# Halving the product of queries and gates in a linear-attention layer

## The chip, the core and the metric

One core of a Trainium2 chip runs the kernel. Its engines are TensorE (PE in the profile; PEld is its weight load), VectorE (DVE), ScalarE (ACT), GpSimd (POOL) and SyncE (SP), which issues the transfers. The metric is the device time of one execution in microseconds (us).

## What is computed

One step of a two-layer decoder trunk over 1024 prompt tokens and 32 sample tokens (8 sequences of 4). Layer 0 is a gated recurrent block, layer 1 an HGRN2 layer: linear attention with a gate for each of the 128 key channels of each of its 8 heads. Cut to what matters here:

```python
def _hgrn2_chunked(q, k, v, log_g, S0):        # for each head
    cum = jnp.cumsum(gc, axis=2)                                     # log gates summed over a chunk's tokens
    inter = jnp.einsum('bhtk,bhkv->bhtv', qc * jnp.exp(cum), S)      # queries decayed from the chunk's start
    attn = jnp.einsum('bhtk,bhsk,bhtsk->bhts', qc, kc, decay)        # decay = exp(cum_t - cum_s), t >= s
    intra = jnp.einsum('bhts,bhsv->bhtv', attn, vc)
    S_new = jnp.exp(last)[..., None] * S + jnp.einsum('bhsk,bhsv->bhkv', kc * jnp.exp(last - cum), vc)

def _hgrn_layer(x, g_norm, w_in, lb, o_gain, w_out, S0):
    q, f, iv, gate = jnp.split(u, 4, axis=-1)                        # u = rmsnorm(x) @ w_in
    q = jax.nn.silu(q)
    log_g = jnp.logaddexp(jnp.log(lbh), jnp.log1p(-lbh) + jax.nn.log_sigmoid(f))
    k = -jnp.expm1(log_g)
```

## The kernel before

Activations lie with channels on the 128 partitions and the 1056 tokens (`TOK`; `HT` is 528, `QT` 264) along the free axis. Matrix products are made of three matmuls each (`mm3`, lines 243 to 245), from a high and a low part of both operands, which ACT and POOL split off (`whi` by a cast, `wlo` by the subtraction on line 323).

**Layer 1, head by head.** For head `h` the input projection gives the queries (row A), the gate (`Gs`, in the buffer named ST), the keys 1 - gate (row B), the values and the output gate. The decayed attention is built by levels of 1, 2, 4 up to 64 tokens. The queries stand in two rows: `arow(h, 0)` as they are, and `arow(h, 1)` multiplied by each token's own gate. `own_gate(h)` makes that second row (the buffer named R) from the first and from Gs in one DVE instruction over all 1056 tokens, line 1064. Then each level multiplies half of a row by the gates up to there (`scale`, lines 1034 and 1043; ACT copies the other half, line 1037), and PE makes the small 32-token blocks of the level from the rows (`diag`, line 1052).

PE's small blocks come in four bursts for each head, `burst1` to `burst4`, between the projection's large products. `burst1(h)` holds `levels01(h)`: 32 products of 32 tokens of row B by both rows A of the same tokens, so it is the first reader of what `own_gate` writes. `burst3(h)` holds `levels816(h)`, whose second part (line 1106) reads rows that `scale` made.

**Heads 0 and 1** are projected in three chunks of 352 tokens (`CH`). Head 0's queries and gates are made as the last work of layer 0 (`first1`, lines 714 to 720), the others by `item` (ACT's tanh on line 1007, POOL's gate and key rows on lines 1010 and 1012, DVE's silu on line 1016). While they run, DVE and POOL also build the sums of activations (`build`, the adds on line 1368) that the later heads' projection uses. **Heads 2 to 7** are projected by `seven`, seven products instead of eight over quarters of 264 tokens: sums of products are collected on DVE in buffers named k (`plus`, line 1501) and finished by `settle`, on ACT (tanh, line 1509; gates, line 1510; tanh of the queries, line 1515) and DVE (line 1516). Large products go to 3 PSUM banks in turn, the small ones to 5.

**What sets the order.** Nothing is issued in the order of the code. Class `Flow` records each operation with its engine, an estimated duration and the keys that it reads and writes; `plan` lays them out engine by engine, by a due time that `back` works out from the plan before, and the best plan of nine is emitted. Here PE's large and small products are one chain whose order is fixed. The others stand where their due times put them, so a change of one operation's cost or keys can move others. Which instruction waits for which is then settled by the regions of the buffers that each reads and writes.

Of the kernel before, what the change touches and what calls it, by code (L numbers as in the profile page):

```python
# [19 lines left out]
ALU = mybir.AluOpType  # L20
# [20 lines left out]
TOK = SEQ + NB * NS  # L41
# [7 lines left out]
HT, QT = TOK // 2, TOK // 4  # L49
# [162 lines left out]
def tile_trunk(ctx: ExitStack, tc: tile.TileContext, xT, prm, hc, w0, wg, wo0, w1, wo1, s_in,  # L212
               yT, h_out, c_out, sp_out, ss_out):
    nc = tc.nc
    V, S, G, T, Q = nc.vector, nc.scalar, nc.gpsimd, nc.tensor, nc.sync
# [80 lines left out]
    with ExitStack() as l0:  # L296
# [18 lines left out]
        def dve(n, emit, r, w, prio=5, both=False):  # L315
            fl.add("DVE", 0.13 + 0.0011 * n, emit, r, w, prio, both=both)
# [610 lines left out]
    with ExitStack() as l1:  # L927
# [27 lines left out]
        Bs, Gs, B2, VT, Gc = a_rows[0], ST, rows[2], rows[0], rows[4]  # L955
# [13 lines left out]
        def arow(h, i):  # L969
            return (R[:, 1], eight("A1")) if i else (R[:, 0 if h % 2 else 2], eight("A", h % 2))  # L970
# [4 lines left out]
        GK = [("G", x) for x in range(4)]  # L975
# [85 lines left out]
        def own_gate(h):  # L1061
            decay[h] = Gs, *GK
            (a, k0), (a1, k1) = arow(h, 0), arow(h, 1)
            dve(TOK, lambda: V.tensor_tensor(a1, a, Gs, op=ALU.mult), (*k0, *GK), k1, 1, True)

        def levels01(h, s, sk):
            av = R[:, 0:2] if h % 2 else R[:, 1:3]
# [450 lines left out]

        dma(si.rearrange("p b v -> p (b v)"), s_in[0], (), two("si"), 4, 512)
        own_gate(0)  # L1520
        spots = [(R[:, 3, i * QT:i * QT + QT], ("tmp", 2 + i)) for i in range(4)]
        small_ = [(tmp[:, i], ("tmp", i)) for i in range(2)]
# [3 lines left out]
        for h in range(HC):  # L1526
            order = [item(h, i) for i in ((0, 1, 3, 2) if h else (3, 2))]
            seq_ = [(i, c) for i in range(len(order)) for c in range(NCH)]
            if h == HC - 1:
                seq_ = seq_[:-6] + [(len(order) - 2 + i, c) for c in (2, 1, 0) for i in (0, 1)]  # L1530
            ws2 = {} if h else ahead
            for n, (i, c) in enumerate(seq_):
                if i not in ws2:
                    ws2[i] = weights(order[i][0], 1024)
                order[i][1](c, *product(ws2[i], xcols(c)))
                if h and n == 5:
                    own_gate(h)
                for j, b in enumerate((burst1, burst2, burst3, burst4)):
                    if n == (SPOTS0, SPOTS)[h][j]:
                        b(h if j < 2 else h - 1)  # L1540
# [15 lines left out]
        for h in range(HC, H):  # L1556
            seven(h, 0, 1, FQ0 if h == HC else FQ, (lambda h=h: burst3(h - 1), lambda h=h: burst4(h - 1)))
            own_gate(h)
            seven(h, 3, 2, GV, (lambda h=h: burst1(h), lambda h=h: burst2(h)))
# [7 lines left out]
        for k in range(H):  # L1567
            if k < 4:
                olds = [("x", 1, k, x) for x in range(2)] + [("T", 1, i, k, x) for i in range(2) for x in range(2)]
            else:  # L1570
                n, i = ((2, 0), (3, 0), (4, 0), (4, 1))[k - 4]
# [241 lines left out]
```

## Time and profile before

| | |
|---|---|
| time, median of 3 runs (lowest, highest) | 1061.53 us (1061.51, 1062.03) |
| profiled execution: its own time, its span | 1061.78 us, 1060.0 us |
| PE busy, share of the span | 1050.5 us, 99% |
| DVE busy | 843.0 us, 80% |
| ACT busy, POOL busy | 588.7 us, 542.4 us |
| mean granted clock of TensorE | 0.996 |
| `own_gate` (line 1064) | 8 instructions, 12.2 us in total |

The span runs from the first to the last instruction; 1.78 us of the execution's own time lie around it. Layer 1 begins at about 500 us of the span, heads 2 to 7 are projected from about 593 to 957 us, and the output projection's end follows. PE matmuls overlap, so a row shows a matmul for longer than the distance to the next one.

### The profile page before, as it was taken

The page shows a single profiled execution, that of the slowest core. Times are in us where ns is not written, and L with a number is a line of the kernel's source. Part 1 is how long each engine was busy: PE and PEld are TensorE (multiplying, and loading weights), DVE is VectorE, ACT ScalarE, POOL GpSimd, SP SyncE. Part 2 cuts the span into 40 slices and gives each one's busy share as a digit, 9 for nine tenths or more (in the row PEclk, how much of TensorE's full clock was granted, in tenths as well). Part 3 has the DMA queues.
Part 4 walks back from the last instruction along what each step waited for, and adds up shares of the span by engine and source line. Part 5 has one row for each costly group of instructions (what it writes and reads, how often), then busy time and mean ns, then how long its engine had stood idle before and what let it go on. Part 6 is the DMA issues. An engine that isn't in the chain of part 4 may idle for free.

```text
span 1060.0 us, 25683 instructions
## 1 busy us (share of the span) xinstructions
PE 1050.5 (99%) x9966; PEld 1024.3 (97%) x9966; DVE 843.0 (80%) x1677; ACT 588.7 (56%) x1329; POOL 542.4 (51%) x604
## 2 busy tenths in 40 slices
PE   9999999999999999999999999999999999999997
PEld 9999999999999999999999999999999999999996
DVE  7999996888888689265799988978979797985435
ACT  6568656877765875243354474646464545652323
POOL 3425443444534366555667555555545565651544
PEclk9999999999999999999999999999999999999998
DMA  9211112123852595440211121212121222355204
GB/s 301 64 27 45 54 51 74 57 61 100 241 157 64 174 298 164 124 136 28 71 47 36 44 101 45 94 42 92 41 86 54 73 71 73 107 177 167 86 1 164
DMA packets 70121, 103.07 MB, mean 97 GB/s; under 512 B 9200, under 2 KB 51184, under 8 KB 70000
## 3 DMA queue, kind: packets, MB, share of 16 engines
q1 hardware_dynamic: 67696, 98.67, 30.0%
q10 hardware_dynamic: 2304, 2.77, 0.8%
q8 instruction: 78, 1.28, 0.5%
q14 instruction: 43, 0.35, 0.1%
HBM read 71.05 MB, written 25.49 MB: 91 GB/s over the span
## 4 chain that ended last, share of the span: by engine, by line
PE 89%; DVE 7%; POOL 1%; DMA 1%; issue 1%; ACT 0%; ACTq 0%; POOLq 0%; DVEq 0%
PE mm L243 24%; PE mm L244 24%; PE mm L245 24%; PE hg L567 1%; PE hg L1052 1%; PE hg L1161 1%; PE hg L1271 1%; DVE R L1368 1%; DMA wraw<-in_w_dram 1%; PE hg L1217 1%; PE hg L243 1%; PE hg L244 1%; PE hg L245 1%; PE hg L1273 1%; DVE tmp L1368 1%
## 5 line engine op out<-in xcount | busy, mean ns | idle before, releaser
L243 PE MATMUL mm<-xh,whi 128*128 128x352 f32 (+1 forms) x1143 | 358.6, 314 | 0.0
L245 PE MATMUL mm<-xh,wlo 128*128 128x352 f32 (+1 forms) x1143 | 353.1, 309 | 0.0
L244 PE MATMUL mm<-xl,whi 128*128 128x352 f32 (+1 forms) x1143 | 353.1, 309 | 0.0
L323 POOL TENSOR_TENSOR wlo<-wraw,whi 128x256 fp32r<-128x256 f32 (+3 forms) x184 | 202.7, 1118 | 178.5 <-ACT whi L378 80.7
L244 PEld LDWEIGHTS mm<-xl,whi 128*128 128x128 f32 x1143 | 215.0, 188 | 1.5
L243 PEld LDWEIGHTS mm<-xh,whi 128*128 128x128 f32 x1143 | 214.7, 188 | 1.5
L245 PEld LDWEIGHTS mm<-xh,wlo 128*128 128x128 f32 x1143 | 214.8, 188 | 0.0
L499 DVE SCALAR_TENSOR_TENSOR k<-xb,prm_sb,k 128x352 f32<-128x352 f32 (+2 forms) x144 | 89.7, 634 | 10.4 <-ACT k L496 5.7
L243 PE MATMUL mm<-t,whi 128*128 128x264 f32 (+1 forms) x306 | 89.3, 292 | 0.0
L244 PE MATMUL mm<-t,whi 128*128 128x264 f32 (+1 forms) x306 | 87.7, 287 | 0.0
L245 PE MATMUL mm<-t,wlo 128*128 128x264 f32 (+1 forms) x306 | 87.5, 286 | 0.0
L1501 DVE TENSOR_TENSOR k<-mm,k 128x264 f32<-128x264 f32 x144 | 60.3, 427 | 20.5 <-PE mm L245 17.4
L323 POOL TENSOR_TENSOR wlo<-R,whi 128x256 fp32r<-128x256 f32 x64 | 60.0, 958 | 24.6 <-ACT whi L1428 24.6
L582 POOL TENSOR_TENSOR k<-X 128x352 f32<-128x352 f32 x36 | 45.8, 1281 | 47.5 <-DVE R L583 38.6
L378 ACT CAST whi<-wraw 128x512 fp32r<-128x512 f32 (+2 forms) x83 | 46.2, 574 | 30.5 <-PE mm L244 19.4
L243 PEld LDWEIGHTS mm<-t,whi 128*128 128x128 f32 x306 | 57.6, 188 | 0.2
L245 PEld LDWEIGHTS mm<-t,wlo 128*128 128x128 f32 x306 | 57.7, 188 | 0.0
L244 PEld LDWEIGHTS mm<-t,whi 128*128 128x128 f32 x306 | 57.6, 188 | 0.0
L1428 ACT CAST whi<-wraw 128x512 fp32r<-128x512 f32 x52 | 32.0, 618 | 36.2 <-PE mm L245 16.7
L243 PE MATMUL mm<-yh,whi 128*128 128x352 f32 x153 | 49.9, 326 | 0.0
L245 PE MATMUL mm<-yh,wlo 128*128 128x352 f32 x153 | 49.4, 323 | 0.0
L244 PE MATMUL mm<-yl,whi 128*128 128x352 f32 x153 | 49.4, 323 | 0.0
(479 smaller groups left out, 2636.5 us busy)
## 6 DMA issues: line engine op xcount, KB each, us to landing
wraw<-in_w_dram SPq DMA_DIRECT2D x90, 256.0 KB, 2.9
wraw<-in_wo_dram SPq DMA_DIRECT2D x34, 192.0 KB, 2.5
si<-in_s_in_dram SPq DMA_DIRECT2D x8, 512.0 KB, 3.6
out_ss_out_dram<-si SPq DMA_DIRECT2D x8, 512.0 KB, 2.6
R<-in_w_dram SPq DMA_DIRECT2D x15, 256.0 KB, 2.6
sg<-x1b SPq DMA_DIRECT2D x21, 176.0 KB, 3.1
x<-sg SPq DMA_DIRECT2D x21, 176.0 KB, 1.8
R<-td SPq DMA_DIRECT2D x72, 44.0 KB, 1.9
```

Source lines behind the costliest of these rows:

```text
L243: T.matmul(out, wh, xh, start=first, stop=False)
L244: T.matmul(out, wh, xl, start=False, stop=False)
L245: T.matmul(out, wl, xh, start=False, stop=last)
L323: emit = lambda: e.tensor_tensor(b, x, a.bitcast(F32), op=ALU.subtract)
L378: act(m, lambda hi=hi, raw=raw, m=m: S.copy(hi[:, :m], raw[:, :m]), rk, (hk,), prio)
L499: dve(u, lambda src=src, dst=dst, sh=sh, k=k: V.scalar_tensor_tensor(dst, sh(src, k), pc("cw", 12 * k + m), dst, op0=ALU.mult, op1=ALU.add ...
L567: fl.add("PE", 0.62, lambda ps=ps, i=i, c=c: T.matmul(ps[:96, :CH], gs[:, i, :], ST[:96, chunk(c)], start=True, stop=True), (("gs",), *((" ...
L582: pool(CH, lambda x=x, a=a, b=b: G.tensor_tensor(x, a.bitcast(F32), b.bitcast(F32), op=ALU.add), (ak, bk), (xk,), 3)
L1052: T.matmul(ps[32 * j:32 * j + 32, n * w:n * w + w], B[:, o:o + 32], q(slice(o, o + 32)), start=True, stop=True, tile_position=(0, 32 * j))
L1368: dve(n, lambda: V.tensor_tensor(o, a, b, op=op), r, (w,), prio, True)
L1428: act(512, lambda: S.copy(hi, raw), (rk,), (hk,), 2)
L1501: dve(QT, lambda: V.tensor_tensor(o[0], z[0], u[0], op=ALU.add), (z[1], u[1]), (o[1],), 0)
```

## The change

`own_gate(h)` becomes two DVE instructions, one for tokens 0 to 527 and one for tokens 528 to 1055. Each is recorded with the keys of its own half: two of the four quarters of the gates, and the same quarters of both query rows. In heads 2 to 7 the quarters have writers of their own, so each half can be placed by itself. In head 1 every chunk of the projection is recorded as writing all quarters, and both halves are recorded behind the last of them. Head 0's rows were written in layer 0's recording, which layer 1's `Flow` does not know.

```diff
         def own_gate(h):
             decay[h] = Gs, *GK
             (a, k0), (a1, k1) = arow(h, 0), arow(h, 1)
-            dve(TOK, lambda: V.tensor_tensor(a1, a, Gs, op=ALU.mult), (*k0, *GK), k1, 1, True)
+            for i in range(2):
+                u = slice(i * HT, i * HT + HT)
+                half = lambda k: [*k[2 * i::4], *k[2 * i + 1::4]]
+                dve(HT, lambda u=u: V.tensor_tensor(a1[:, u], a[:, u], Gs[:, u], op=ALU.mult), (*half(k0), *GK[2 * i:2 * i + 2]), half(k1), 1, True)
```

The three added lines shift the lines below: the new instructions are on line 1067, and what was line 1501 is line 1504.

PE's order is the same in both programs. On DVE, where head 0's rows come in at the end of layer 0 (line 715 finishes the last chunk of its queries; ST is the gate, line 1043 begins the products of neighbouring gates), before and after the change:

```order
L715 SCALAR_TENSOR_TENSOR R<-R,mm 128x352
L1064 TENSOR_TENSOR R<-R,ST 128x1056
L961 MEMSET ssq 128x9
L1043 TENSOR_TENSOR sg<-ST 128x528
L1043 TENSOR_TENSOR sg<-sg 128x264
```

```order
L1067 TENSOR_TENSOR R<-R,ST 128x528
L715 SCALAR_TENSOR_TENSOR R<-R,mm 128x352
L1067 TENSOR_TENSOR R<-R,ST 128x528
L961 MEMSET ssq 128x9
L1043 TENSOR_TENSOR sg<-ST 128x528
```

The first half went ahead of the last chunk of the queries, and the second half stands where the whole stood.

On DVE in head 1 (line 1368, later 1371, is `build`'s adds, line 1016 the silu of a chunk of the output gate, read from PSUM, line 1056 keeps a level's blocks), before and after:

```order
L1368 TENSOR_TENSOR tmp<-tmp,xl 128x264
L1064 TENSOR_TENSOR R<-R,ST 128x1056
L1043 TENSOR_TENSOR sg<-ST 128x528
L1016 SCALAR_TENSOR_TENSOR sg<-k,mm 128x352
L1043 TENSOR_TENSOR sg<-sg 128x264
L1056 COPY_PREDICATED attnd<-mask_86,hg 128x256
```

```order
L1371 TENSOR_TENSOR tmp<-tmp,xl 128x264
L1067 TENSOR_TENSOR R<-R,ST 128x528 x2
L1016 SCALAR_TENSOR_TENSOR sg<-k,mm 128x352
L1043 TENSOR_TENSOR sg<-ST 128x528
L1043 TENSOR_TENSOR sg<-sg 128x264
L1056 COPY_PREDICATED attnd<-mask_86,hg 128x256
```

Both halves stand in the place of the whole, and the silu came ahead of the first product of gates.

On DVE in head 4, which stands for heads 3 to 6 (line 1501, later 1504, takes a large product out of PSUM into k; line 1516, later 1519, finishes the second half of the queries; line 1438, later 1441, combines weights), before and after:

```order
L1501 TENSOR_TENSOR k<-mm,k 128x264
L1516 SCALAR_TENSOR_TENSOR R<-R,k 128x264
L1120 COPY attn<-mm 64x4x64
L1438 TENSOR_TENSOR wraw<-wraw 128x512
L1516 SCALAR_TENSOR_TENSOR R<-R,k 128x264
L1064 TENSOR_TENSOR R<-R,ST 128x1056
L1501 TENSOR_TENSOR k<-mm,k 128x264
L1043 TENSOR_TENSOR sg<-ST 128x528
```

```order
L1504 TENSOR_TENSOR k<-mm,k 128x264
L1067 TENSOR_TENSOR R<-R,ST 128x528
L1519 SCALAR_TENSOR_TENSOR R<-R,k 128x264
L1123 COPY attn<-mm 64x4x64
L1519 SCALAR_TENSOR_TENSOR R<-R,k 128x264
L1067 TENSOR_TENSOR R<-R,ST 128x528
L1441 TENSOR_TENSOR wraw<-wraw 128x512
L1504 TENSOR_TENSOR k<-mm,k 128x264
L1043 TENSOR_TENSOR sg<-ST 128x528
```

The first half went ahead of the two pieces of the second half's queries, the second half stands right behind them, and the weights' combination moved behind it; the next product is taken out of PSUM behind the same work as before.

## The prediction

> **What bounds the kernel now.** I read the page first, then the busy time by stretches of layer 1, then the waits of PE and of its weight load, then the chain of work that ended last.
>
> ```profile
> PE 1050.5 (99%) x9966; PEld 1024.3 (97%) x9966; DVE 843.0 (80%) x1677; ACT 588.7 (56%) x1329; POOL 542.4 (51%) x604
> ```
>
> PE is busy for 99% of the span. The question is therefore not how much work DVE is spared, but where PE still waits for it. The stretches of layer 1 (heads 0 and 1, heads 2 to 7, the last bursts, the end), with columns length, PE, PEld, DVE, ACT, POOL:
>
> ```profile
> 500.00:590.00 90.00, 88.97 (x1095) 86.57 (x1094) 78.31 (x150) 37.56 (x89) 60.42 (x58) 1.00 0.15 46
> 590.00:957.00 367.00, 367.00 (x5167) 354.16 (x5166) 318.45 (x685) 201.63 (x534) 207.99 (x239) 1.00 0.25 81
> 957.00:985.00 28.00, 28.00 (x197) 27.62 (x197) 13.20 (x34) 6.73 (x17) 7.43 (x10) 1.00 0.46 142
> 985.00:1060.00 75.00, 67.69 (x431) 64.92 (x429) 35.80 (x82) 24.36 (x63) 36.95 (x40) 0.94 0.26 87
> ```
>
> PE misses 1.03 us in heads 0 and 1, nothing in heads 2 to 7, and 7.31 us at the very end, where the product is no longer made. The waits of PE, and of its weight load, from 500 to 985 us (total, times, longest):
>
> ```profile
> PE hg L1106 <- DVE a L1034: 0.5, 1, 0.5
> PE hg L1052 <- DVE R L1064: 0.4, 1, 0.4
> ...
> PEld hg L1052 <- DVE R L1064: 0.7, 1, 0.7
> PEld hg L1106 <- ACT a L1037: 0.6, 1, 0.6
> PEld hg L1052 <- POOL a L1012: 0.3, 1, 0.3
> ```
>
> Two places are left: I call them place A (line 1106, head 0's third burst) and place B (line 1052, head 1's first burst). At B the weight load waits twice, first for the product and then for POOL's last piece of the key row. The weight-load rows add up to 1.6 us. The change can hardly give back more, since no other wait of PE in this layer has work of the product behind it. The chain of waits shows what stands behind both places:
>
> ```profile
> 511.13 1.31 DVE R L1064
> ...
> 539.90 0.60 DVE a L1034
> ...
> 564.97 2.42 POOL a L1012
> ...
> 567.43 0.47 PE hg L1052 x18
> ...
> 687.90 1.03 PE hg L1052 x64
> ...
> 744.60 1.03 PE hg L1052 x64
> ...
> 801.30 1.03 PE hg L1052 x64
> ```
>
> From 511.13 us, head 0's product, the chain runs on DVE to 557.5 us, then on POOL, and only at 567.43 comes back to PE. From there on it is PE. The last three rows are `burst1` of heads 3 to 5: 56.70 us from one to the next, twice to 0.01 us. Nothing that jitters sets that pace.
>
> **The change part by part.** *The two instructions.* The whole and, as the nearest shape, another product of two SBUF rows over 528 tokens (least, median and greatest ns):
>
> ```profile
> L1064 DVE TENSOR_TENSOR R<-R,ST x8: 1247/1681/1682, 511.1 to 908.9; 128x1056 f32<-128x1056 f32 x8
> L1043 DVE TENSOR_TENSOR sg<-ST x8: 697/784/1045, 512.4 to 911.4; 128x528 f32<-128x528 f32 x8
> ```
>
> Two halves cost 2 x 0.70 - 1.25 = 0.15 us more than one whole, both undisturbed, up to 2 x 1.05 - 1.25 = 0.85 us if both are disturbed. Over eight heads DVE gets 1.2 us more work (to 6.8 us). In heads 2 to 7 it has 367.00 - 318.45 = 48.55 us without work, which covers either end.
>
> *Place A, head 0.* DVE's and POOL's rows around the product, with the idle time before each in brackets:
>
> ```profile
> 503.14 0.53 DVE L323 TENSOR_TENSOR xl<-sg,xh 128x352 fp32r<-128x352 f32 x1 [1.46 <-ACT xh L459]
> 506.88 0.52 DVE L715 SCALAR_TENSOR_TENSOR R<-R,mm 128x352 f32<-128x352 f32 x1 [3.21 <-ACT R L714]
> 511.13 1.31 DVE L1064 TENSOR_TENSOR R<-R,ST 128x1056 f32<-128x1056 f32 x1 [3.74 <-POOL ST L720]
> 503.09 1.01 POOL L720 TENSOR_SCALAR ST<-k,smalls 128x352 f32<-128x352 f32 x1
> 510.46 0.64 POOL L720 TENSOR_SCALAR ST<-k,smalls 128x352 f32<-128x352 f32 x1 [0.70 <-ACT k L718]
> ```
>
> The first half needs the gates of the first two chunks, there at 504.10. In the new order it stands ahead of line 715, in DVE's 3.21 us without work, so it is done by about 505 us, even at 1.05 us. That cover would have to shrink to a third before it cost anything. Only the second half waits for POOL at 511.1. There DVE now spends 0.70 us instead of 1.31; POOL's neighbour runs beside either, and cost the whole 1.31 - 1.25 = 0.06, so I take 0.76 and DVE is 0.55 us ahead (bounds 1.31 - 1.05 = 0.26 and 0.61). DVE's queue is full from there to place A: in the new order the same adds and level products stand ahead of the row that PE waits for, some in another sequence. What else could end last there is ACT's copy of the same rows, which waits for the same DVE queue. PE's wait of 0.50 us falls to nothing; at the other end, if something between absorbs the lead, it stays, and if a step like the first row's were placed ahead of the level products, it would grow by that step's 0.53 us.
>
> *Place B, head 1.* DVE, POOL and PE:
>
> ```profile
> 565.17 1.25 DVE L1064 TENSOR_TENSOR R<-R,ST 128x1056 f32<-128x1056 f32 x1
> 566.34 0.70 DVE L1043 TENSOR_TENSOR sg<-ST 128x528 f32<-128x528 f32 x1
> 567.07 0.52 DVE L1016 SCALAR_TENSOR_TENSOR sg<-k,mm 128x352 f32<-128x352 f32 x1
> 564.15 0.81 POOL L1010 TENSOR_SCALAR ST<-k,smalls 128x352 f32<-128x352 f32 x1
> 564.95 2.43 POOL L1012 TENSOR_SCALAR a<-k,smalls 128x352 f32<-128x352 f32 x1
> 566.47 1.44 PE L1052 MATMUL hg<-R,a 128*32 128x64 f32 x62 [0.43 <-DVE R L1064]
> ```
>
> The first half reads no token of the last chunk. It ends at about 565.9, and PE's first 16 small products need no more, so PE begins about 0.6 us earlier. By itself this is worth nothing: from the 23rd product on (token 704, 22 x 32) PE reads the last chunk of the key row, which POOL ends at 567.38, and that end decides. POOL's instruction takes 2.43 us, its like beside free DVE 0.64 (the row at 510.46). It ends 0.34 us after DVE's two products of SBUF rows, which end at 567.04. In the new order the halves end at about 566.5 and then comes the silu, which reads one operand from PSUM. If POOL gets through then, it ends at 566.8, 0.55 us earlier; if it doesn't, nothing is gained, and the extra 0.15 us of DVE is lost. I take 0.4.
>
> The two held each other up here: POOL's 2.43 us began at 564.95, ahead of both of DVE's products, and ended behind both. The Trainium skill, SBUF — State Buffer, section Who interferes with whom, says that the one that issues first has the shared port for its whole instruction and the other is fully blocked. By the starts that the profile shows, the trace does not agree: POOL was first and waited. By the rule POOL's instruction would go between the halves, and the sum would be 0.7 us instead of 0.9 (worked out as the second rival).
>
> *Heads 2 to 7.* In the new order the first half is done while the last queries are still being made. But PE asks for it late:
>
> ```profile
> 738.62 1.68 DVE L1064 TENSOR_TENSOR R<-R,ST 128x1056 f32<-128x1056 f32 x1
> 740.34 0.43 DVE L1501 TENSOR_TENSOR k<-mm,k 128x264 f32<-128x264 f32 x1
> 742.98 0.28 PE L243 MATMUL mm<-t,whi 128*128 128x264 f32 x1
> ```
>
> The whole ended at 740.30, and `burst1` began at 744.60. PE already has the row 4.30 us too early; having it earlier still is worth zero. The cost is zero too: the next product is taken out of PSUM at 740.34, ending at 740.77, and PE wants that bank at 742.98, so it may come 2.21 us later. What stands ahead of it grew by 0.15 us. Rows that changed places on ACT, POOL and SP (weights' casts and subtractions, level copies, loads near the end) I cost at nothing: PE waits for none of them now, and they moved by a few rows.
>
> *The sum.* 0.50 at A and 0.40 at B is 0.9 us, against the profiled execution's 1061.78 (span 1060.0): 1060.9. The runs' median is 0.25 below that execution, so 1061.53 - 0.9 = **1060.6 us**. A difference within 0.2% (2.1 us: below 1059.4 is faster, above 1063.7 slower) is about what a measurement of this kernel can tell from no change.
>
> **The rivals.**
>
> *The lead is lost on the way* (1061.5, chance 0.25). Between 511 and 567 us the chain passes to ACT and POOL at 557.5 us, and DVE's other inputs may come no earlier. For it speaks that place B ends with POOL; against it that the chain has DVE back to back for 46 us. Both waits stay: 1061.53 less nothing.
>
> *POOL gets in between the halves* (1060.8, chance 0.16). At B, POOL's 0.64 us would lie between them, and the second half would end at 565.17 + 0.70 + 0.64 + 0.70 = 567.2 instead of 566.5. PE would stop there instead of at POOL, 0.2 us before the old 567.4, so 0.7 instead of 0.9. The rows at place B speak against it: there POOL let two of DVE's products in a row go first. By the Trainium skill's rule (SBUF — State Buffer, Who interferes with whom), weighed there, this is the likely course.
>
> *Slower: products leave PSUM too late in heads 2 to 7* (1063.9 and more, chance 0.06). Both halves and the moved weights' combination stand ahead of the evacuation, and each can be held up by POOL by 1.68 - 1.25 = 0.43 us. Three of them make 1.3 us, still below the 2.21 of slack, so it takes another cause on top. From 2.21 us on PE waits in every head: at 2.6 us late it is 0.4 x 6 = 2.4 us in all.
>
> *Faster by more: waits that a busy PE hides* (1058.3, chance 0.02). The weight load is idle for 367.00 - 354.16 = 12.84 us in heads 2 to 7; if `burst1`, one of four bursts, waited for the product in a quarter of it, 3.2 us could go. The equal steps of 56.70 us and the weight load's list, with line 1064 in it once, speak against it. The Trainium skill, Perfetto Trace Analysis, section Identifying the Most-Contended Engine, calls matmul busy time a bad measure of the distance to the limit and points to the weight load's; by it the 12.84 us are room.
>
> That the change does something else than it says I exclude: PE's order is the same, and the order shows 16 halves.
>
> **How the numbers follow.** The forecast has 0.51 (1060.6), the rivals 0.25, 0.16, 0.06 and 0.02. Below, the range takes in the full 1.6 us of the waits: 1059.9. Above, no gain and the 0.5 us between the highest and lowest run: 1062.0. With a little for other runs' scatter I give 1059.8 to 1062.2; it leaves out the last two rivals. The chances are 0.02 faster, 0.92 within 0.2%, 0.06 slower.
>
> **What would show it.** Right: the wait of line 1106 is gone or under 0.1 us; the first half of head 0 starts near 504 us; POOL's last piece of head 1's key row (line 1015) takes under 2.1 us; `burst1` still comes every 56.70 us. Wrong: a wait of PE in heads 2 to 7, steps over 56.8 us, or place A unchanged although head 0's second half took 0.8 us or less.

## The result and the profile after

The changed kernel took 1063.03 us (median of 20 runs, 1062.33 to 1064.36) against 1061.68 (20 runs, 1061.04 to 1062.28) for the kernel before on the same chip: 1.35 us more, ratio 1.0014 with a 95% interval of 1.0008 to 1.002. The forecast was 0.9 us less, and the value lies above the range. It is still within the 0.2% that the prediction set as the limit of what can be told from no change, but the interval leaves no doubt of the sign. The profiled execution took 1062.84 us, its span 1061.1. Three executions in the runs below took 1301 to 2633 us, one of them the profiled one of its kernel; the ratios leave them out.

The page of the changed kernel, engines' busy time:

```profile
PE 1050.4 (99%) x9966; PEld 1023.8 (96%) x9966; DVE 849.8 (80%) x1685; ACT 587.7 (55%) x1329; POOL 541.0 (51%) x604
```

PE does the same work. DVE, with eight instructions more, is busy 6.8 us longer. That this is also the upper end of what the prediction gave the halves is chance: the runs below show that it is not the halves that take it. The stretches with heads 0 and 1 and with heads 2 to 7 (length, then PE, PEld, DVE, ACT, POOL):

```profile
500.00:590.00 90.00, 89.96 (x1102) 87.69 (x1101) 79.03 (x153) 38.25 (x90) 60.38 (x58) 1.00 0.14 46
590.00:957.00 367.00, 365.39 (x5139) 352.07 (x5139) 324.07 (x688) 199.43 (x530) 205.22 (x239) 1.00 0.24 81
```

In the first, PE misses 0.04 us instead of 1.03: places A and B gave back 0.99 us, as forecast. In the second it misses 1.61 us where it missed nothing. The waits of PE from 590 to 985 us (total, times, longest):

```profile
PE mm L243 <- DVE k L1504: 0.9, 4, 0.2
PE hg L1052 <- issue: 0.7, 1, 0.7
```

Both are new: four times PE waits with a large product until DVE has read another out of the PSUM bank, and once it stands still for nothing that the profile shows. The chain of waits carries the same (start, us, what):

```profile
698.66 0.66 PE hg L1052 x48
...
742.61 0.89 DVE sg L1043
...
751.55 1.82 DVE wraw L1441
...
755.83 0.66 PE hg L1052 x48
...
813.02 0.66 PE hg L1052 x48
...
814.25 0.74 issue
...
871.14 0.66 PE hg L1052 x48
```

From one head's burst to the next it is now 57.17, 57.19 and 58.12 us instead of 56.70, and in each of heads 3 to 6 the chain, which was PE's alone there, goes over DVE's gate levels and one combination of weights (the rows at 742.61 and 751.55 are head 4's).

What the wait looks like in head 4. DVE before, then PE before (start, us, engine, line, operation, idle time before it in brackets):

```profile
752.03 0.43 DVE L1501 TENSOR_TENSOR sg<-mm,k 128x264 f32<-128x264 f32 x1 [0.34 <-PE mm L245]
752.38 0.42 DVE L1501 TENSOR_TENSOR k<-mm,k 128x264 f32<-128x264 f32 x1
752.72 1.38 DVE L1438 TENSOR_TENSOR wraw<-wraw,R 128x512 f32<-128x512 f32 x1
...
754.75 0.29 PE L243 MATMUL mm<-t,whi 128*128 128x264 f32 x1
```

And after:

```profile
751.46 1.91 DVE L1441 TENSOR_TENSOR wraw<-wraw,R 128x512 f32<-128x512 f32 x1
...
753.64 0.42 DVE L1504 TENSOR_TENSOR k<-mm,k 128x264 f32<-128x264 f32 x1
...
753.62 0.28 PE L245 MATMUL mm<-t,wlo 128*128 128x264 f32 x1
754.11 0.39 PE L243 MATMUL mm<-t,whi 128*128 128x264 f32 x1 [0.21 <-DVE k L1504]
```

Before, DVE waited for PE, read the bank by 752.80, and PE came for it 1.95 us later. After, PE would have begun at 753.74 (0.12 us behind the matmul at 753.62), but the read ends at 754.06, 0.32 too late. DVE lost 2.27 us against PE. Matching the starts of the matmuls in the two traces one by one, PE falls back by 0.49, 0.47, 0.49 and 0.49 us at this product of heads 3 to 6, by 0.95 us at the issue stall, and had gained 1.05 at A and B. (The waits in PE's rows are shorter, since a row shows a matmul for longer than the distance to the next one.)

### The profile page after: what moved, and what is told of

The parts are those of the page before. It is cut to its first block, busy times and chain, and to the rows that moved or that the text cites. A ratio compares the mean times of both kernels' runs of the same rounds, so it can differ in the third digit from the quotient of the medians.

```text
span 1061.1 us, 25679 instructions
## 1 busy us (share of the span) xinstructions
PE 1050.4 (99%) x9966; PEld 1023.8 (96%) x9966; DVE 849.8 (80%) x1685; ACT 587.7 (55%) x1329; POOL 541.0 (51%) x604
## 4 chain that ended last, share of the span: by engine, by line
PE 90%; DVE 7%; DMA 1%; issue 1%; ACT 0%; POOL 0%; ACTq 0%; POOLq 0%; DVEq 0%; SPq 0%
PE mm L243 25%; PE mm L244 25%; PE mm L245 25%; PE hg L567 1%; PE hg L1052 1%; PE hg L1274 1%; PE hg L1220 1%; PE hg L243 1%; PE hg L244 1%; PE hg L245 1%; PE hg L1276 1%; PE hg L1164 1%; DVE sg L1043 1%; PE mm L1052 1%; DVE k L1504 1%
## 5 line engine op out<-in xcount | busy, mean ns | idle before, releaser
L323 POOL TENSOR_TENSOR wlo<-R,whi 128x256 fp32r<-128x256 f32 x64 | 57.8, 923 | 19.5 <-ACT whi L1431 19.4
```

The source lines that it names most:

```text
L323: emit = lambda: e.tensor_tensor(b, x, a.bitcast(F32), op=ALU.subtract)
```

## The experiments

The first theories: **1**, the planner put one combination of weights (line 1441) ahead of two PSUM reads, as the rows above show, and that alone delays them; **2**, the halves are the cost, by DVE's extra work. What the first expectation calls theory 3, on the stall, is taken up in the last section; in the later ones theories 3 to 5 are those that came out of the runs. The kernels are measured against the one before, on the same chip.

**The change again**, without an edit.

> The changed kernel once more, as the anchor for the others and as a second profile. Theory 1 (the planner moved the next head's first combination of weights ahead of two PSUM reads of DVE, and PE then waits for those reads): the four waits of line 243 for DVE line 1504 stand again in heads 3 to 6, 0.9 us in all as PE's own rows count them and about 1.85 us by the offset of PE's rows, and the time is 1.2 to 1.4 us above the kernel before. Theory 2 (the second instruction itself is the cost, by DVE's extra 0.85 us per head and by POOL beside it): the same total. Theory 3: the one stall of 0.7 us marked issue in head 5 belongs to the program; then it stands again at the same product. If it is scatter of one execution, it is gone and the last PE row comes about 0.5 us earlier against the runs' median.

1063.11 us against 1061.80, ratio 1.0012 (1.0003 to 1.0021). The four waits are there again, and the stall too, shorter. In heads 3 and 6 PE now waits some 10 us later, for another read, and falls back by 0.7 us:

```profile
PE mm L243 <- DVE k L1504: 1.3, 4, 0.4
PE hg L1052 <- issue: 0.3, 1, 0.3
```

**Heads 0 and 1 alone.**

```diff
+            if h < HC:     # HC = 2
+                for i in range(2):
...
+            else:
+                dve(TOK, lambda: V.tensor_tensor(a1, a, Gs, op=ALU.mult), (*k0, *GK), k1, 1, True)
```

> Halves in heads 0 and 1 alone, the whole product in heads 2 to 7. Theory 1: DVE's order in heads 3 to 7 is again that of before, so no wait of PE in heads 2 to 7, while the two waits at places A and B stay away: 0.50 + 0.40 (up to 1.2 by the offset of PE's rows) below the kernel before, so 0.9 to 1.2 us below it. Theory 2 gives the same sign here, since six of the eight second instructions are gone. Rival of the prediction (the lead at A and B is lost on the way): no difference from the kernel before.

1060.36 us against 1061.80: 1.4 us less, a little more than expected, ratio 0.9987 (0.9978 to 0.9996). PE waits nowhere between 500 and 985 us:

```profile
500.00:590.00 90.00, 90.00 (x1102) 87.75 (x1102) 79.15 (x153) 37.86 (x90) 60.39 (x58) 1.00 0.14 46
590.00:957.00 367.00, 367.00 (x5169) 354.36 (x5168) 320.38 (x688) 202.41 (x537) 206.40 (x239) 1.00 0.25 82
```

The gain at A and B is real; this version beats both kernels.

**Heads 2 to 7 alone**, the same edit with the condition turned round.

> The other part: halves in heads 2 to 7 alone, the whole product in heads 0 and 1. Theory 1 and theory 2 both: the waits at places A and B are there as before (0.5 and 0.4 us), the four waits of heads 3 to 6 too, and the time is 1.85 us above the kernel before (2.4 us if the stall marked issue is caused by the halves). If the loss of the changed kernel came from heads 0 and 1 (another order of level products there), this kernel would be level with the one before.

1063.76 us, 2.0 more than before, ratio 1.0018 (1.0009 to 1.0028). The old waits and the new ones stand side by side:

```profile
PE mm L243 <- DVE k L1507: 1.1, 4, 0.4
PE hg L1112 <- DVE a L1034: 0.5, 1, 0.5
PE hg L1052 <- DVE R L1070: 0.4, 1, 0.4
```

1.4 us gained in heads 0 and 1 and 2.0 lost in the rest make 0.6; the change and its second run lose 1.3. The 0.7 between them is inside the intervals, and the stall, which neither part shows, is of that size.

**The combination put back.** The changed kernel; in heads 3 to 6 the one combination stands behind the two reads again.

```diff
+        order = self.moved(list(best[3]))     # takes one operation behind another in the finished plan
+        fl.moves = [(("combine", h + 1, 0), ("last", h, 2, 0), "behind") for h in range(HC, H - 1)]
```

> The changed kernel with halves in all heads, but in heads 3 to 6 the next head's first combination of weights stands behind the two PSUM reads that it had been moved ahead of. Nothing else in DVE's order differs. Theory 1: the four waits of PE go, bursts come every 56.70 us again, and with the gain at A and B the time is 0.9 to 1.2 us below the kernel before, about 2 us below the changed one. Theory 2: the halves are still there with all their extra work, so half or more of the 1.85 us stays, and the time is within 0.4 us of the kernel before or above it.

1062.99 us, 1.2 more than before, ratio 1.0011 (1.0002 to 1.002): no better than the change. Theory 1, by which that one row is the whole cause, fell. One more run of the same kernel (1063.78 us), with a profile, was to show where the wait had gone.

> One look with a profile at the kernel whose time came out level with the changed one (1.2 us above before, where theory 1 gave 0.9 to 1.2 below). Theory 1 as it was put is thereby wrong or incomplete. Two things it can be: (a) the wait moved on: PE does not wait for the two reads of the fifth product any more, but for another read of PSUM or for the weights that now come 0.85 us later, again some 0.45 us in each of heads 3 to 6; (b) the combination was never the cause: line 243 still waits for the same reads, 4 times 0.2 to 0.4 us, because DVE is late by the halves themselves (theory 2).

The waits, and then DVE and PE in time (line 1522 is here what was 1504, line 258 what was 243):

```profile
PE mm L258 <- DVE k L1522: 1.7, 4, 0.4
```
```profile
765.16 0.43 DVE L1522 TENSOR_TENSOR k<-mm,k 128x264 f32<-128x264 f32 x1
...
765.64 0.39 PE L258 MATMUL mm<-xh,whi 128*128 128x264 f32 x1 [0.42 <-DVE k L1522]
```

Case (a): the reads 753 us into the span are in time, and PE waits 11 us later for another, which in the trace of before ended at 762.84, 2.0 us ahead of PE's matmul at 764.87. PE falls back by 0.67 to 0.71 us there in each of heads 3 to 6, more than in the changed kernel, but the stall is absent, so the times come out level. DVE is late as a whole, and the one row only chose where PE notices.

**The combination moved in the old order**, the reverse: before, with the whole product and that one row ahead of the reads.

```diff
+        fl.moves = [(("combine", h + 1, 0), ("value", h, 5, 0), "ahead") for h in range(HC + 1, H - 1)]
```

> The kernel before with its whole product, but in heads 3 to 6 the next head's first combination of weights stands ahead of the two PSUM reads of the fifth product, as in the changed kernel. In the profile of before those reads start at 751.69 in head 4 and the combination takes 1.38 to 1.9 us, so they end at 753.9 to 754.4, and PE wants the bank at 754.74. Theory 1 alone (the moved combination is enough): waits of 0.2 to 0.5 us in heads 3 to 6, 0.8 to 1.9 us slower than before. Theory 2 (the second instruction makes DVE late): the reads still end 0.3 us ahead of PE, no wait and no difference from before.

1063.29 us, ratio 1.0015 (1.0006 to 1.0024). In the profile the heads come every 56.91 us instead of 56.70, and the issue stall of head 5 is there (0.4 us). 0.2 us for each head is less than half of what the change loses there. In this execution PE was already 0.9 us late ahead of layer 1, which leaves 1.0 of the span's 1.9 us for what follows. One moved row does a part, without any half.

**Halves in the old order**: both instructions are recorded as one operation at the place of the whole, and every engine keeps its order. Only in head 0 do they not run there together: in the trace the first half starts at 503.90 us, ahead of line 715, as in the changed kernel.

```diff
-            dve(TOK, lambda: V.tensor_tensor(a1, a, Gs, op=ALU.mult), (*k0, *GK), k1, 1, True)
+            dve(TOK, lambda: [V.tensor_tensor(a1[:, u], a[:, u], Gs[:, u], op=ALU.mult) for u in (slice(0, HT), slice(HT, TOK))],
+                (*k0, *GK), k1, 1, True)
```

> The order of before on every engine, with the product as two instructions of 528 tokens at the place of the whole. Theory 1 (the order is the cause): no wait in heads 2 to 7; at place A the second half alone waits for POOL's gates, which gives the 0.5 us back, at place B little or nothing, so 0.5 to 0.9 us below the kernel before. Theory 2 (the halving costs by itself): the waits of line 243 for line 1501 appear in heads 3 to 6, 0.45 us each, and the time is 0.9 to 1.4 us above before.

1060.80 us against 1061.80, ratio 0.9989 (0.9979 to 0.9998), and no wait of PE from 500 to 985 us: place B gained too, where little or nothing was expected. Theory 2 fell. What is left is theory **3**: the new order of DVE's other rows costs, whatever is halved. The fourth corner is that order with a whole product.

**The new order with the whole product**, at the second half's place.

```diff
-                dve(HT, lambda u=u: V.tensor_tensor(a1[:, u], a[:, u], Gs[:, u], op=ALU.mult), ...
+                dve(HT, lambda i=i: i and V.tensor_tensor(a1, a, Gs, op=ALU.mult), ...
```

> The fourth corner of order and halving: the order of the changed kernel on every engine, but the whole product in one instruction at the place of the second half. Theory 3 (the new order of DVE's other work is the cost; the halves are not): waits of PE in heads 3 to 6 as in the changed kernel, steps of some 57.2 us between bursts, DVE over 55 us busy per head; place A waits again (no early half), so the time is level with the changed kernel or up to 0.5 us slower: 1.2 to 2.0 us above before. Theory 2 (the halves cost by themselves): steps of 56.70 us and a time within 0.4 us of before.

1063.73 us against 1061.59: 2.1 more, just above what was expected, ratio 1.0019 (1.001 to 1.0028). PE waits four times for line 1504 as in the changed kernel, and at place B for the whole product, 0.6 us. The same head of the four corners (before, halves in the old order, the change, whole in the new order; DVE's busy time is the third after the length):

```profile
744.60:801.30 56.70, 56.70 (x810) 54.82 (x813) 47.61 (x105) 30.68 (x80) 31.61 (x37) 1.00 0.21 68
```
```profile
743.30:800.00 56.70, 56.70 (x813) 54.82 (x815) 47.23 (x106) 30.68 (x80) 32.71 (x37) 1.00 0.21 68
```
```profile
743.60:800.80 57.20, 56.99 (x813) 54.90 (x817) 49.51 (x106) 30.37 (x80) 31.14 (x38) 1.00 0.20 68
```
```profile
744.60:801.80 57.20, 56.99 (x810) 54.90 (x814) 49.51 (x105) 30.21 (x80) 31.55 (x38) 1.00 0.21 68
```

(The expectations' 55.5 and 53.4 us add up the rows, each of which overlaps the next a little; the windows count the overlap once.) Halving changes DVE's time by -0.4 and 0.0 us, the order by +1.9 (with the whole product) and +2.3 (with halves). Theory 3 holds.

**POOL's share.** DVE has the same instructions in both orders, so what grew are their durations. The changed kernel with POOL's subtractions in heads 2 to 7 made for 16 of each 256 columns; the rest of the low parts is left out:

```diff
-                    subtract(G, 512 // CUT, lo[:, w], raw[:, w], hi[:, w], (rk, hk), (lk,), 2)
+                    pool(512 // CUT, lambda v=slice(w.start, w.start + (16 if h >= HC else 512 // CUT)): G.tensor_tensor(
+                        lo[:, v], raw[:, v], hi[:, v].bitcast(F32), op=ALU.subtract), (rk, hk), (lk,), 2)
```

> The changed kernel with the same order on every engine, but in heads 2 to 7 POOL makes the low parts of the weights for 16 of each 256 columns; the rest is left out. Theory 4 (in the new order more of DVE's instructions with two SBUF operands run beside POOL's, and this is the 2.2 us that DVE is busier per head): DVE's busy time per head falls from 55.5 to below 53.4, the waits of PE in heads 3 to 6 are gone, steps of 56.70 us, and with the gain at places A and B the time is 0.9 to 1.4 us below before. Rival (the sequence by itself makes DVE late, POOL has no part): DVE's instructions get shorter by less than 1 us per head, and waits of 0.2 to 0.5 us in heads 3 to 6 stay.

1060.57 us against 1061.59, ratio 0.9987 (0.9979 to 0.9996), with no wait of PE from 500 to 985 us. By itself this proves little, since DVE is spared 6.5 us in each head, three times what the order costs. The busy times have to be compared with the same edit in the kernel before:

> The kernel before (whole product, old order), with POOL's subtractions in heads 2 to 7 shortened as in the run of the changed kernel: 16 of each 256 columns, the rest left out. Busy time of DVE in a head, by the windows: before 47.6 us, changed 49.5, changed with POOL short 42.97. Theory 4 (the 1.9 us between the two orders are DVE held up by POOL, no more): here 42.5 to 43.0, level with the changed one but for the 0.15 us of the second half. Rival (the new order costs DVE something by itself): 41 to 42, a gap of 1 us or more is left.

1061.68 us against 1062.11, one run of each. DVE's busy time in the head, changed order and old order with POOL short:

```profile
743.90:800.70 56.80, 56.80 (x814) 54.92 (x817) 43.01 (x106) 30.65 (x80) 15.92 (x37) 1.00 0.20 68
```
```profile
744.30:801.00 56.70, 56.70 (x807) 54.82 (x807) 43.02 (x105) 30.51 (x79) 16.26 (x37) 1.00 0.21 68
```

43.01 and 43.02: with most of POOL's work gone the two orders cost DVE the same, to within the 0.15 us expected of the second half. So the 1.9 us between them are DVE held up by POOL. Which rows are held up, over heads 3 to 5 of before, of the changed kernel, and of the changed one with POOL short (count, total us, mean ns, idle before):

```profile
L1438 DVE TENSOR_TENSOR wraw<-wraw 128x512 f32<-128x512 f32 x10 | 8.4, 835 | 0.2
L1043 DVE TENSOR_TENSOR sg<-ST 128x528 f32<-128x528 f32 x3 | 2.3, 783 | 0.0
```
```profile
L1441 DVE TENSOR_TENSOR wraw<-wraw 128x512 f32<-128x512 f32 x10 | 10.2, 1016 | 0.2
L1043 DVE TENSOR_TENSOR sg<-ST 128x528 f32<-128x528 f32 x3 | 3.9, 1292 | 0.0
```
```profile
L1441 DVE TENSOR_TENSOR wraw<-wraw 128x512 f32<-128x512 f32 x10 | 6.9, 688 | 0.2
L1043 DVE TENSOR_TENSOR sg<-ST 128x528 f32<-128x528 f32 x3 | 2.1, 699 | 0.0
```

Combinations and gate levels, both with two operands in SBUF, take 0.69 and 0.70 us when POOL is short, more in the old order, and most in the new one. Together they grew by 3.4 us over the three heads, 1.1 of the 1.9 us per head; other rows grew as well, and some fell (the 15 level products of 512 tokens on line 1034 from 0.79 to 0.68 us each). The Trainium skill, SBUF — State Buffer, section Who interferes with whom, says that a DVE instruction with two SBUF inputs contends with a POOL instruction that reads SBUF; these rows agree.

**The slack measured**: before, with the product made twice in heads 2 to 7.

```diff
-            dve(TOK, lambda: V.tensor_tensor(a1, a, Gs, op=ALU.mult), (*k0, *GK), k1, 1, True)
+            dve(TOK, lambda: [V.tensor_tensor(a1, a, Gs, op=ALU.mult) for _ in range(2 if h >= HC else 1)], (*k0, *GK), k1, 1, True)
```

> The order of before, with the whole product made twice in a row in heads 2 to 7 (the second writes the same values): 1.25 to 1.7 us more for DVE in each head, at the place where the prediction counted 2.21 us of slack and 48.55 us without work. The prediction's own step: no wait, no difference from before, or 0.2 us. Theory 5 (DVE has no idle time from there to 766 us, so what is added ahead of 740 is still late at the reads 12 and 24 us later, whose slack is 1.9 and under 1 us): PE waits in heads 2 to 6, 0.3 to 0.9 us each, 1.5 to 4 us above before.

1066.01 us against 1061.59: 4.4 more, above the 1.5 to 4 expected, ratio 1.004 (1.0027 to 1.0052). The same waits stand in the same heads, the stall too, and one more at 938 us, where PE waits for the low part of an activation (line 323):

```profile
PE mm L243 <- DVE k L1501: 1.3, 4, 0.3
...
PE mm L244 <- DVE xl L323: 0.5, 1, 0.5
PE hg L1052 <- issue: 0.5, 1, 0.5
```

DVE's extra time at the product is not covered. It also grew on the way: the second read of head 4 that started at 752.38 before started at 755.81 here, with PE 1.07 us later by then, so DVE lost 2.36 us, more than the 1.25 to 1.7 that were added. The trace of before shows why nothing was made up, in four stretches from one head's burst into the next head:

```profile
687.90:710.00 22.10, 22.10 (x370) 21.47 (x369) 20.91 (x50) 9.79 (x22) 12.32 (x15) 1.00 0.10 30
710.00:738.60 28.60, 28.60 (x392) 27.49 (x391) 20.79 (x46) 18.47 (x53) 14.38 (x17) 1.00 0.25 85
738.60:757.60 19.00, 19.00 (x335) 18.59 (x333) 18.11 (x35) 8.79 (x19) 12.19 (x15) 1.00 0.18 56
757.60:766.70 9.10, 9.10 (x91) 8.74 (x85) 8.69 (x24) 3.42 (x8) 5.03 (x7) 1.00 0.15 41
```

From the product to 766.70 DVE is idle for 1.30 us of 28.10; the largest part of its idle time, 7.81 us, lies between 710 and 738.6, ahead of the product. Theory **5** holds: what makes DVE later in the full half reaches PE there, less the 2 us of slack at the reads.

## Why the prediction was wrong

*Places A and B: right, in size and, but for the silu at B, in mechanism.* In the changed kernel (DVE and POOL):

```profile
503.74 0.71 DVE L1067 TENSOR_TENSOR R<-R,ST 128x528 f32<-128x528 f32 x1 [0.47 <-POOL ST L720]
...
510.74 0.76 DVE L1067 TENSOR_TENSOR R<-R,ST 128x528 f32<-128x528 f32 x1 [3.74 <-POOL ST L720]
...
564.13 1.31 DVE L1067 TENSOR_TENSOR R<-R,ST 128x528 f32<-128x528 f32 x2
...
563.91 1.88 POOL L1012 TENSOR_SCALAR a<-k,smalls 128x352 f32<-128x352 f32 x1
```

The first half of head 0 starts near 504 us, the second takes the 0.76 us put down for it, and POOL's last piece (on line 1012 still, not 1015) fell from 2.43 to 1.88 us, under the 2.1 that was named. 0.9 us was forecast, the windows show 0.99. One detail at B was not needed: the prediction let POOL through while the silu runs, but with halves in the old order, where the first product of gates comes ahead of the silu, POOL's piece took 1.88 us as well and place B gained as much. With the whole product and the silu ahead of it POOL's piece took 1.89, but PE waited for the product instead. The halves gave the gain. The rival that the lead is lost on the way is out by this. So is the one that POOL gets in between the halves: they take 1.31 us together, back to back, with POOL's instruction, begun 0.22 us earlier, again the one held up.

*Heads 2 to 7: wrong.* The step that failed is "The cost is zero too". It let DVE's work ahead of the next read grow by 0.15 us and gave the rows that changed places on ACT, POOL and SP nothing, because "PE waits for none of them now, and they moved by a few rows"; DVE's own moved rows got a price only in a rival, 0.43 us each. In its place the runs showed that PE falls back by 0.47 to 0.49 us in each of four heads, 1.9 us in all, and by the stall. Three things were wrong in the step.

- The moved rows have a price. Their places set which of them fall beside POOL's work, and that made DVE 1.9 us busier in each head. A moved row can also simply stand ahead of a read: the one combination alone cost 0.2 us per head. How the loss divides between longer rows and rows ahead of a read, and which engine's moved rows weigh most, no run separates. The term put down for the halves, 0.15 to 0.85 us per head, was by contrast too high: -0.4 and 0.0.
- The cover was an average. "48.55 us without work, which covers either end" is true of heads 2 to 7 as a whole, but most of it lies ahead of the product. Behind it DVE is full for 28 us, and what is late stays late.
- The slack was read at one place only, the read right behind the product. Its 2.21 us is of the right size, for the later reads have 1.95 and 2.0; but to meet it a delay has to be summed up over all rows until there.

*The rival "products leave PSUM too late in heads 2 to 7"* is what happened, with a loss near its 0.4 us a head (0.47 to 0.49 in four heads, not six). It was held back at 0.06 because it takes "another cause on top", and that cause, the moved rows, had been given a price of nothing shortly before. The named signs of being wrong, a wait of PE in heads 2 to 7 and steps over 56.8 us, both came.

*The issue stall* was in no case. It makes up 0.3 to 0.7 us of the loss by PE's rows, 0.55 and 0.95 by the matched starts.

*The rival of waits that a busy PE hides* is out: with halves in all heads in the old order, and no wait of PE left, the steps stay at 56.70 us.

## What to carry to other kernels

Where a planner decides the order, a change of one operation is a change of all rows that move with it; price those rows too, above all two-operand DVE rows that may come to lie beside POOL. Look for an engine's idle time in the stretch between the change and the next reader that can be late, not over the whole stage, and sum the delay up to that reader. And an edit whose gain lies in two of eight heads is better made in those two, or without letting the rest of the plan move.

## What the runs showed of the hardware

**A stall of PE that goes with a late instruction fetch.** The stall marked issue came behind one and the same matmul, the 124th of head 5's second burst. The transfers of before in a window of 1.6 us from 810.6 (40 slices of 0.04 us; the queue's packets, MB and share), and the burst's first matmuls:

```profile
GB/s 0 0 0 0 0 410 0 0 0 0 0 0 0 0 0 0 0 0 0 0 0 0 0 0 0 0 0 0 0 0 0 0 0 0 0 0 0 0 0 0
...
q8 instruction: 1, 0.02, 4.8%
```
```profile
813.00 0.51 PE L1052 MATMUL hg<-R,a 128*32 128x32 f32 x35
```

The same of the changed kernel, the window from 812.2:

```profile
GB/s 0 0 0 410 0 0 0 0 0 0 0 0 0 0 0 0 0 0 0 0 0 0 0 0 0 0 0 0 0 0 0 0 0 0 0 0 0 0 0 0
...
q8 instruction: 1, 0.02, 4.7%
```
```profile
812.95 0.55 PE L1052 MATMUL hg<-R,a 128*32 128x32 f32 x40
...
814.99 0.26 PE L1052 MATMUL hg<-R,sg 128*32 128x32 f32 x6 [0.74 <-issue]
```

Each window holds one packet of 16 KB on the instruction queue q8, the one that moves most, which is taken here for PE's. Before, it began at 810.80, 2.2 us ahead of the burst, and the burst ran through. In the changed kernel it began at 812.33, 0.6 us ahead, and took 1.2 us; PE got through some 120 small matmuls in 1.3 us and then stood still until 814.99. Twelve profiles (all but the one of 1301 us) go the same way: with 0.6 to 0.8 us of lead there is a stall of 0.3 to 0.7 us (the change and its second run, the moved combination in the old order, the whole in the new order, the product twice), with 1.9 us or more there is none. In the five, PE goes on 1.3 to 1.5 us behind the packet's end, each time; in the other seven the same matmul comes 1.9 us or more behind it. The Trainium skill, Runtime: NRT & Kernel Launch, section Instruction fetch mechanics, says that the sequencer fetches the next 16 KiB while it executes, and that this is mostly hidden. The trace agrees with the size of the blocks; if the fetch is what stopped PE, it was not hidden in a burst of very short matmuls. That the late fetch is the cause rests on this match alone, since no run changed the fetch. What made it late is open: in the changed kernel the only other packet from 808 to 816 us is one of 8 KB on the other instruction queue, at 809, which before has too, and two kernels with like waits of PE were spared.

**What the meeting of DVE and POOL is worth.** With POOL's subtractions cut to a sixteenth of their columns, DVE's busy time per head fell by 4.6 us in the old order (47.6 to 43.0) and by 6.5 in the new one. In which order the two meet is worth 1.9 us per head here, at equal work. Either can be the one held up: at place B POOL's piece took 1.88 us while both halves beside it took 1.31, and in heads 3 to 5 DVE's first product of gates took 1.29 us instead of 0.70. Why the new order meets worse, row by row, was not taken apart.
